# First two panels' weights in quarters ahead of their activations, and fixed orders on three engines up to the first norm's factors

## The chip, the cores and the metric

The kernel runs on one core of one Trainium2 chip. The metric is the device time of one execution in microseconds (us). The kernel before took 930.16 us (median of 3 runs, 929.11 to 930.49). TensorE is written PE below, VectorE DVE, ScalarE ACT, GpSimd POOL, and the queue that issues most transfers SP.

## The reference, cut to what matters

One layer of a hybrid decoder for 512 prompt tokens and 8 sample tokens that share the weights, all in float32. What this study touches is the first norm, the first columns of the input projection, and the rotary step on them:

```python
def rmsnorm(x, g):
    xf = x.astype(jnp.float32)
    y = xf * lax.rsqrt(jnp.mean(xf * xf, axis=-1, keepdims=True) + EPS)
    return (y * g.astype(jnp.float32)).astype(x.dtype)

def project(u, w_in, w_gk2, b_gk, pos):
    ...
    qa, ka, va, qb, kb, vb, rb, glr, ga, gb = jnp.split(u @ w_in, offs, axis=-1)
    qa = rope(qa.reshape(b, t, A_HEADS, A_HEAD_DIM), pos)
    ka = rope(ka.reshape(b, t, A_HEADS, A_HEAD_DIM), pos)
    ...
    qa, ka, va, qb, kb, vb, gk, rb, ga, gb = project(rmsnorm(xp, g_norm1[l]), w_in[l], w_gk2[l], b_gk[l], pos_p)
```

After that come windowed attention, a gated linear attention, an output projection, a second norm and a feed-forward block, none of which the change touches.

## The kernel before, in words

The 520 tokens (512 and 8) stand in columns, in two halves of 260; the 1024 features stand in 8 slices of 128 partitions, one slice being `k`. All weights are cut into panels of 128 output features; a panel is 8 tiles of 128 by 128, 512 KB, and its product is 48 matmuls: 8 slices, 2 halves, and 3 passes. The passes come from a split of every float32 operand into a high part (`whi`, `uh`) and a rest (`wlo`, `ul`): high by high, high by rest, rest by high. ACT makes the high part of a weight piece and DVE the rest (`split_piece`, L80 and L81; a piece is 4 tiles, half a panel), and the matmuls of a panel are issued by `k_tile` (L129).

The norm is not applied to the activations before the matmul. `start` multiplies the raw activations `xr` by the norm's gain only and splits them (L237 on ACT, L238 on DVE), and the matmuls of panels 0 and 1 run slice by slice as data arrive. The factor of each token, `rb`, is computed beside that in `stats`: 8 squares on ACT (L263), 7 adds on DVE (L267), a matmul with ones that sums over the partitions (L269, tile `rps`), and in `rsqrt` a logarithm and an exponential on ACT (L193, L195) with four steps of refinement on DVE (L194, L196, L197, L198). `rb` is multiplied in after the product.

Panels 0 and 1 are the two halves of the first key heads, 2 and 3 those of the first query heads, 4 and 5 the first values. `rope_pair` takes two products from PSUM: four multiplies by the cosine and sine tables (L303, L306 of the first panel, L309, L310 of the second, tile `rt`), a subtraction and an addition (L313, tile `ro`), for the keys the multiplication by `rb` (L315), and eight transfers into `KTt` or `QTt` that SP issues (L317). After the keys, `rb` is multiplied into both tables (L330), so that later pairs need no factor of their own.

Two limits of storage set the order of the work around the change. Products of panels go to the PSUM pool `pm` with two buffers (panel 2 alone has its own): panels 0, 1, 3, 4, 5 take them in turn, so panel 3 needs panel 0's product read, panel 4 panel 1's, and panel 5 that of panel 3, by its L309 and L310. Raw panels have two buffers, so the load of panel `i + 2` (L72) waits until DVE has made the last rest of panel `i`. The split weights have four buffers of half a panel, so a piece of panel `i` waits for the matmuls of panel `i - 2`.

The order of instructions on each engine is made by a scheduler that follows priorities and its own timeline. `behind` adds a constraint of order that is no wait; `after` adds a wait on a semaphore.

Of the kernel before, what the change touches and what calls it, by code (L numbers as in the profile page):

```python
# [18 lines left out]
D = 1024  # L19
# [5 lines left out]
KT = 8  # L25
# [19 lines left out]
class Build:  # L45
# [31 lines left out]
    def split_piece(self, raw, x, n, dst=None):  # L77
        nc = self.nc
        hi, lo = dst or (self.wp.tile([P, n, P], F32R, tag=t, name=t, bufs=self.wbufs) for t in ("whi", "wlo"))
        nc.scalar.activation(hi, raw[:, x:x + n], AF.Copy)  # L80
        nc.vector.tensor_tensor(lo, raw[:, x:x + n], hi.bitcast(F32), op=ALU.subtract)  # L81
        return hi, lo

    def split_panel(self, i):
# [3 lines left out]
        self.split[i] = [self.split_piece(raw, x, min(4, kt - x),  # L88
                                          i in self.wdst and [t[:, x:x + min(4, kt - x)] for t in self.wdst[i]])
                         for x in range(0, kt, 4)]  # L90
# [6 lines left out]
    def start_panels(self, panels):  # L97
        self.panels, self.raw, self.split, self.wdst, self.cur = panels, {}, {}, {}, 0
# [87 lines left out]
    def rsqrt(self, pool, out, ss, n, scale, np_=P):  # L186
# [6 lines left out]
        nc.scalar.activation(a[:np_], ss, AF.Ln, scale=scale, bias=self.eps[:np_])  # L193
        nc.vector.tensor_scalar(v[:np_], ss, scale, EPS, op0=ALU.mult, op1=ALU.add)  # L194
        nc.scalar.activation(out, a[:np_], AF.Exp, scale=-0.5)  # L195
        nc.vector.tensor_tensor(a[:np_], out, out, op=ALU.mult)  # L196
        nc.vector.scalar_tensor_tensor(a[:np_], a[:np_], -0.5, v[:np_], op0=ALU.mult, op1=ALU.mult)  # L197
        nc.vector.scalar_tensor_tensor(out, a[:np_], 1.5, out, op0=ALU.add, op1=ALU.mult)  # L198
# [7 lines left out]
    def start(self):  # L206
# [7 lines left out]
        raw = [self.raw_tile(i) for i in range(2)]  # L214

        def weights(x):
            for i in range(2):
                nc.sync.dma_start(raw[i][:, x:x + 4], self.panels[i][0][:, x:x + 4])

        nc.sync.dma_start(xr[:, 0], I["xT"][:, 0])  # L220
        weights(0)
        nc.sync.dma_start(xr[:, 1], I["xT"][:, 1])
        nc.sync.dma_start(xr[:, 2:4], I["xT"][:, 2:4])
        weights(4)
        for a in (4, 6):
            nc.sync.dma_start(xr[:, a:a + 2], I["xT"][:, a:a + 2])
# [3 lines left out]
        self.keep_warm(10)  # L230
# [5 lines left out]
        for k in range(KT):  # L236
# [977 lines left out]
```

## Time and profile before

| what | us |
|---|---|
| median of 3 runs | 930.16 |
| the profiled execution's own time | 930.86 |
| its span, first to last instruction | 929.1 |
| PE busy | 911.9 |
| DVE busy | 549.7 |
| ACT busy | 379.9 |

The span is the time between the first and the last instruction on the core in one profiled execution; the rest of its own time, 1.76 us, lies around it. Busy time of PE includes the pipelined tails of matmuls, so it is an upper account of its work. A line of the timeline stands for one instruction or for several like ones in a row: its start, the time until the last of them ends, the engine, the line of the code, what is written from what, and in brackets the idle time of the engine ahead of it and what ended that. In a row of the waits, the time is that in which the engine ahead of the arrow stood idle until the one behind it was done.

### The profile page before, as it was taken

To read this page: it belongs to the slowest core of one execution; us is meant where nothing else is said; L and a number is where in the kernel's file an instruction comes from. 1 tells how busy PE (TensorE), PEld (TensorE's weight loads), DVE (VectorE), ACT (ScalarE), POOL (GpSimd) and SP (SyncE) were. 2 spreads that over 40 slices of the span, in tenths; PEclk is the share of its full clock that TensorE was granted. 3 is DMA by queue.
4 is the path that set the end of the run, shared out by engine and by line. 5 is a ranking of instruction groups with operands and counts; after the bars stand their busy time and mean duration, and the time that the engine had idled before them with its cause. 6 is when DMAs were issued, how large, how long until landed. Compare 5 with 4: busy or idle time off the path is not lost.

```text
span 929.1 us, 19801 instructions
## 1 busy us (share of the span) xinstructions
PE 911.9 (98%) x8286; PEld 890.0 (96%) x8286; DVE 549.7 (59%) x1078; ACT 379.9 (41%) x735; POOL 66.1 (7%) x119
## 2 busy tenths in 40 slices
PE   9999999999999999999999999999999999999995
PEld 9999999999999989989999999999999999999995
DVE  6856656774966858585755555433443344555654
ACT  6234323452644445664633444322432243225432
POOL 1000000000110102010000000000000000000000
PEclk9999999999999999999999999999999999999998
DMA  7556464223544534212777767777774222223301
GB/s 250 184 180 205 128 224 174 96 75 135 205 139 141 199 104 138 74 48 98 273 272 272 272 227 273 272 272 273 272 273 159 92 91 92 91 92 114 114 32 61
DMA packets 37291, 155.27 MB, mean 167 GB/s; under 512 B 5145, under 2 KB 11553, under 8 KB 35250
## 3 DMA queue, kind: packets, MB, share of 16 engines
q1 hardware_dynamic: 32210, 95.26, 29.4%
q0 software_dynamic: 4848, 58.73, 17.8%
q8 instruction: 65, 1.06, 0.5%
q14 instruction: 24, 0.20, 0.1%
q10 hardware_dynamic: 144, 0.01, 0.0%
HBM read 140.66 MB, written 54.17 MB: 210 GB/s over the span
## 4 chain that ended last, share of the span: by engine, by line
PE 94%; DVE 2%; DMA 2%; SPq 1%; issue 0%; ACT 0%; DVEq 0%; ACTq 0%
PE mps L129 80%; PE mps L1046 5%; PE sps L384 1%; DMA QTt<-ro 1%; PE pvp L417 1%; PE lev L618 1%; PE gpo L705 1%; PE gpu L709 1%; PE ptp L401 1%; PE vps L349 1%; PE gso L772 1%; PE gpo L707 1%; DMA raw<-in_w_in 1%; SPq L317 1%; PE mps L582 0%
## 5 line engine op out<-in xcount | busy, mean ns | idle before, releaser
L80 ACT ACTIVATE whi<-raw 128x512 fp32r<-128x512 f32 x264 | 165.9, 630 | 360.8 <-PE mps L129 325.2
L81 DVE TENSOR_TENSOR wlo<-raw,whi 128x512 fp32r<-128x512 f32 x264 | 182.7, 693 | 149.4 <-ACT whi L80 145.7
L129 PE MATMUL mps<-uh,whi 128*128 128x260 f32 x928 | 193.0, 288 | 1.9 <-DVE rt L310 1.1
L129 PE MATMUL mps<-ul,whi 128*128 128x260 f32 x928 | 192.5, 286 | 0.0
L129 PE MATMUL mps<-uh,wlo 128*128 128x260 f32 x928 | 190.4, 285 | 0.0
L129 PEld LDWEIGHTS mps<-uh,whi 128*128 128x128 f32 x928 | 143.6, 189 | 4.9 <-ACT whi L80 2.4
L129 PEld LDWEIGHTS mps<-ul,whi 128*128 128x128 f32 x928 | 144.3, 189 | 2.0 <-issue 1.2
L129 PEld LDWEIGHTS mps<-uh,wlo 128*128 128x128 f32 x928 | 143.8, 188 | 1.4 <-issue 0.9
L129 PE MATMUL mps<-hh,wlo 128*128 128x260 f32 x512 | 103.2, 283 | 0.0
L129 PE MATMUL mps<-hh,whi 128*128 128x260 f32 x512 | 103.2, 283 | 0.0
L129 PE MATMUL mps<-hl,whi 128*128 128x260 f32 x512 | 103.0, 283 | 0.0
L129 PEld LDWEIGHTS mps<-hh,whi 128*128 128x128 f32 x512 | 79.0, 188 | 0.1
L129 PEld LDWEIGHTS mps<-hh,wlo 128*128 128x128 f32 x512 | 78.9, 188 | 0.0
L129 PEld LDWEIGHTS mps<-hl,whi 128*128 128x128 f32 x512 | 78.7, 188 | 0.0
L129 PE MATMUL mps<-fh,wlo 128*128 128x260 f32 x384 | 77.3, 283 | 0.0
L129 PE MATMUL mps<-fl,whi 128*128 128x260 f32 x384 | 77.2, 283 | 0.0
L129 PE MATMUL mps<-fh,whi 128*128 128x260 f32 x384 | 76.8, 282 | 0.0
L129 PEld LDWEIGHTS mps<-fh,wlo 128*128 128x128 f32 x384 | 59.2, 188 | 0.0
L129 PEld LDWEIGHTS mps<-fl,whi 128*128 128x128 f32 x384 | 59.0, 188 | 0.0
L129 PEld LDWEIGHTS mps<-fh,whi 128*128 128x128 f32 x384 | 59.0, 188 | 0.0
L1046 PE MATMUL mps<-fh,lw 128*128 128x260 f32 x256 | 46.6, 283 | 0.0
L1046 PEld LDWEIGHTS mps<-fh,lw 128*128 128x128 f32 x256 | 39.6, 188 | 0.1
(334 smaller groups left out, 1290.0 us busy)
## 6 DMA issues: line engine op xcount, KB each, us to landing
raw<-in_w_in SPq DMA_DIRECT2D x56, 512.0 KB, 3.5
raw<-in_w_up SPq DMA_DIRECT2D x32, 512.0 KB, 4.3
raw<-in_w_down SPq DMA_DIRECT2D x32, 512.0 KB, 4.7
sx<-in_state SPq DMA_DIRECT2D x8, 512.0 KB, 4.5
sx<-dV SPq DMA_DIRECT2D x8, 512.0 KB, 4.8
out_sgla<-sx POOLq DMA_DIRECT2D x8, 512.0 KB, 6.0
raw<-in_w_pb SPq DMA_DIRECT2D x8, 512.0 KB, 6.0
raw<-in_w_o SPq DMA_DIRECT2D x8, 512.0 KB, 6.0
```

Source lines behind the costliest of these rows:

```text
L80: nc.scalar.activation(hi, raw[:, x:x + n], AF.Copy)
L81: nc.vector.tensor_tensor(lo, raw[:, x:x + n], hi.bitcast(F32), op=ALU.subtract)
L129: self.last = self.nc.tensor.matmul(o[:, :HC], wt, x[:, k, j * HC:(j + 1) * HC], start=(k == 0 and n == 0), stop=(k == kt - 1 and n == 2))
L317: nc.sync.dma_start(dst[64 * (h % 2) + 32 * x:64 * (h % 2) + 32 * x + 32, gi * 2 + h // 2, :], o[32 * h:32 * h + 32, :])
L349: nc.tensor.transpose(pt[:, r * P:(r + 1) * P], vt[:, r * P:(r + 1) * P], self.c["ident"])
L384: m = nc.tensor.matmul(pss[hh][:, hp, c], Q[rows, i, b * P:(b + 1) * P], K[rows, i, ks], start=True, stop=True)
L401: nc.tensor.transpose(pt[:, hh, x], prs[hp][:, hh, x * P:(x + 1) * P], self.c["ident"])
L417: m = nc.tensor.matmul(po[64 * hh:64 * hh + 64, hp * P:(hp + 1) * P], v, pTs[hp][:, hh, x], start=(x == first), stop=(x == 1))
L618: self.nc.tensor.matmul(ps[32 * i:32 * i + 32, c], k[:, 32 * b:32 * b + 32], q[:, n * b:n * b + n], start=True, stop=True)
L705: nc.tensor.matmul(po[:, :256], ST[:, c], V[:, c], start=True, stop=(c == 0))
L707: nc.tensor.matmul(po[:, :256], qe[:, c * P:(c + 1) * P], st, start=False, stop=True)
L1046: nc.tensor.matmul(ps, w, x[:, kk, cc], start=(kk == 0 and n == 0), stop=(kk == KT - 1 and n == 2))
```

## The change

The load order on SP becomes: for each pair of slices, a quarter (2 tiles, 128 KB) of panel 0's and of panel 1's weights, then the two slices of activations one by one (the last two in one transfer). Before, halves of the panels and single or double slices alternated. ACT and DVE split the quarters as they come, so that `start` has 8 pieces of the two panels where it had 4. Eight matmuls warm PE up where ten did. In `start` the matmuls of a slice go pass by pass over both panels (high by high, rest by high, high by rest). The squares and adds move from `stats` into `start`. The helper `pin` puts every listed instruction behind the one before it on its engine, and at the end of the first `proj_qk` three written sequences carry the order on: ACT up to the first piece of panel 4, DVE through the factors' refinement, and PE, where the summing matmul stands ahead of slice 6 of panel 2 (`self.third`).

```diff
     def split_piece(self, raw, x, n, dst=None):
...
-        nc.scalar.activation(hi, raw[:, x:x + n], AF.Copy)
-        nc.vector.tensor_tensor(lo, raw[:, x:x + n], hi.bitcast(F32), op=ALU.subtract)
+        self.piece = (nc.scalar.activation(hi, raw[:, x:x + n], AF.Copy),
+                      nc.vector.tensor_tensor(lo, raw[:, x:x + n], hi.bitcast(F32), op=ALU.subtract))
...
+                if self.cur == 3 and k == 6 and n + j == 0:
+                    self.third = self.last
...
-        def weights(x):
+        last = {}
+
+        def pin(engine, m):
+
+            if engine in last:
+                self.behind(m, last[engine])
+            last[engine] = m
+
+        def load(o, i):
+            pin("SP", nc.sync.dma_start(o, i))
+
+
+        for y in range(0, KT, 2):
             for i in range(2):
-                nc.sync.dma_start(raw[i][:, x:x + 4], self.panels[i][0][:, x:x + 4])
-
-        nc.sync.dma_start(xr[:, 0], I["xT"][:, 0])
-        weights(0)
-        nc.sync.dma_start(xr[:, 1], I["xT"][:, 1])
-        nc.sync.dma_start(xr[:, 2:4], I["xT"][:, 2:4])
-        weights(4)
-        for a in (4, 6):
-            nc.sync.dma_start(xr[:, a:a + 2], I["xT"][:, a:a + 2])
+                load(raw[i][:, y:y + 2], self.panels[i][0][:, y:y + 2])
+            for k in ((y, y + 1), (y + 1, y + 2)) if y < KT - 2 else ((y, y + 2),):
+                load(xr[:, k[0]:k[1]], I["xT"][:, k[0]:k[1]])
...
-        self.keep_warm(10)
+        self.keep_warm(8)
...
+        def square():
+            k = len(sqs)
+            sqs.append(ap.tile([P, NT], F32, tag="sq", name="sq", bufs=6))
+            self.squared = nc.scalar.activation(sqs[k], xr[:, k], AF.Square)
+            pin("ACT", self.squared)
+
+        def add(k):
+            self.added = nc.vector.tensor_tensor(sqs[0], sqs[0], sqs[k], op=ALU.add)
+            pin("DVE", self.added)
+
+        for y in range(0, KT, 2):
             for i in range(2):
...
+                self.split_piece(raw[i], y, 2, [t[:, y % 4:y % 4 + 2] for t in w[i][-1]])
+                for e, m in zip(("ACT", "DVE"), self.piece):
+                    pin(e, m)
+            if y == 6:
+                square()
+                add(2)
+            for k in (y, y + 1):
+                self.split_x = nc.scalar.activation(self.uh[:, k], xr[:, k], AF.Copy, scale=self.g("n1", k))
+                pin("ACT", self.split_x)
...
+                for n in (0, 2, 1):
+                    for i in range(2):
+                        wt, x = self.passes(w[i], k, self.uh, self.ul)[n]
+                        for j in range(2):
...
+                            pin("PE", self.last)
+            if y < 6:
+                square()
+            if y == 2:
+                add(1)
+        add(3)
+        square()
+        square()
+        add(4)
...
         with self.tc.high_priority():
-            self.split_panel(2)
...
+            for x in (0, 4):
+                self.split[2].append(self.split_piece(self.raw2, x, 4))
+                for e, m in zip(("ACT", "DVE"), self.piece):
+                    pin(e, m)
+            for k in (6, 7):
+                square()
+            for k in (5, 6, 7):
+                add(k)
...
+            (a3, d3), (b3, e3) = self.pieces[3]
+            (ln, ex), m = self.rs
+
+            for seq in ([self.squared, a3, b3, ln, ex, self.pieces[4][0][0]],
+                        [self.added, *self.rt[:2], d3, m[0], e3, *m[1:], *self.rt[2:], self.pieces[4][0][1]], [self.summed, self.third]):
+                for x, y in zip(seq[1:], seq):
+                    self.behind(x, y)
```

What follows shows how the instructions stand in a row on two engines; numbers of buffers are kept where rows would read alike. On DVE, from the second multiply of the key pair's second panel to the finished factors (`rb_290`), before:

```order
L310 TENSOR_TENSOR rt_317<-mps_111,cs_242 128x520
L81 TENSOR_TENSOR wlo_411<-raw_343,whi_410 128x512
L81 TENSOR_TENSOR wlo_415<-raw_343,whi_414 128x512
L313 TENSOR_TENSOR ro_322<-rt_314,rt_316 128x512
L313 TENSOR_TENSOR ro_322<-rt_314,rt_316 128x8
L313 TENSOR_TENSOR ro_331<-rt_317,rt_315 128x512
L313 TENSOR_TENSOR ro_331<-rt_317,rt_315 128x8
L194 TENSOR_SCALAR rv_291<-rps_96 128x520
L196 TENSOR_TENSOR ra_292<-rb_290 128x520
L81 TENSOR_TENSOR wlo_490<-raw_408,whi_489 128x512
L197 SCALAR_TENSOR_TENSOR ra_292<-ra_292,rv_291 128x520
L198 SCALAR_TENSOR_TENSOR rb_290<-ra_292,rb_290 128x520
```

The same stretch of DVE now, where L345 and L348 are the four multiplies (L303, L306 of panel 0, `mps_117`, and L309, L310 of panel 1, `mps_118`, before), and L198 to L202 are the refinement:

```order
L345 TENSOR_TENSOR rt_326<-mps_117,cs_271 128x520
L345 TENSOR_TENSOR rt_327<-mps_117,sn_272 128x520
L81 TENSOR_TENSOR wlo_358<-raw_277,whi_357 128x512
L198 TENSOR_SCALAR rv_303<-rps_105 128x520
L81 TENSOR_TENSOR wlo_362<-raw_277,whi_361 128x512
L200 TENSOR_TENSOR ra_304<-rb_302 128x520
L201 SCALAR_TENSOR_TENSOR ra_304<-ra_304,rv_303 128x520
L202 SCALAR_TENSOR_TENSOR rb_302<-ra_304,rb_302 128x520
L348 TENSOR_TENSOR rt_328<-mps_118,sn_272 128x520
L348 TENSOR_TENSOR rt_329<-mps_118,cs_271 128x520
```

The refinement moved ahead of panel 1's multiplies, of the sums (L313) and of the rests of panel 4, with the two rests of panel 3 around its first step.

On DVE, the last rows up to the reading of panel 3's product (`mps_430`) now, where L353 is L313 of before, L370 is L330 and L355 is L315:

```order
L353 TENSOR_TENSOR ro_343<-rt_329,rt_327 128x8
L370 TENSOR_TENSOR cs_271<-cs_271,rb_302 128x520
L81 TENSOR_TENSOR wlo_506<-raw_420,whi_505 128x512
L355 TENSOR_TENSOR ro_334<-ro_334,rb_302 128x512
L355 TENSOR_TENSOR ro_334<-ro_334,rb_302 128x8
L355 TENSOR_TENSOR ro_343<-ro_343,rb_302 128x512
L355 TENSOR_TENSOR ro_343<-ro_343,rb_302 128x8
L345 TENSOR_TENSOR rt_414<-mps_365,cs_271 128x520
L345 TENSOR_TENSOR rt_415<-mps_365,sn_272 128x520
L81 TENSOR_TENSOR wlo_572<-raw_499,whi_571 128x512
L348 TENSOR_TENSOR rt_416<-mps_430,sn_272 128x520
L348 TENSOR_TENSOR rt_417<-mps_430,cs_271 128x520
```

Here the order is nearly as before: the tables, the multiplication by `rb` and the query pair's multiplies still follow each other, all behind the factors, with one table and two rests at other places among them.

On PE, around the matmuls that sum over the partitions, before (`mps_353` is panel 2, `mps_418` panel 3):

```order
L129 MATMUL mps_353<-uh_79,whi_252 128x260 x2
L129 MATMUL mps_353<-ul_80,whi_252 128x260 x2
L129 MATMUL mps_353<-uh_79,wlo_253 128x260 x2
L269 MATMUL rps_96<-sq_265,ones_94 128x260 x2
L129 MATMUL mps_418<-uh_79,whi_345 128x260 x2
L129 MATMUL mps_418<-ul_80,whi_345 128x260 x2
```

The same place on PE now (`mps_365` is panel 2, `mps_430` panel 3):

```order
L131 MATMUL mps_365<-uh_82,whi_283 128x260 x2
L131 MATMUL mps_365<-ul_83,whi_283 128x260 x2
L131 MATMUL mps_365<-uh_82,wlo_284 128x260 x2
L318 MATMUL rps_105<-sq_155,ones_103 128x260 x2
L131 MATMUL mps_365<-uh_82,whi_283 128x260 x2
L131 MATMUL mps_365<-ul_83,whi_283 128x260 x2
```

The sums moved from behind the last slice of panel 2 to ahead of its slice 6.

## Rows read from the trace of the kernel before

**Rows 1.** The page: span, busy times by engine, granted clock of 40 slices.
```profile
span 929.1 us, 19801 instructions
...
PE 911.9 (98%) x8286; PEld 890.0 (96%) x8286; DVE 549.7 (59%) x1078; ACT 379.9 (41%) x735; POOL 66.1 (7%) x119
...
PEclk9999999999999999999999999999999999999998
```
**Rows 2.** Waits of PE: total us, times, longest us.
```profile
PE sps L384 <- DMA QTt<-ro: 1.5, 1, 1.5
PE mps L129 <- DVE rt L310: 1.1, 1, 1.1
```
**Rows 3.** Timeline of PE: the start, panel 2's first matmuls, the sums, panel 5's first.
```profile
1.06 4.63 PE L255 MATMUL rps<-ones 128*128 128x128 f32 x20 [1.06 <-DVE eps L232]
5.34 0.78 PE L129 MATMUL mps<-uh,whi 128*128 128x260 f32 x2
...
7.35 0.50 PE L129 MATMUL mps<-uh,whi 128*128 128x260 f32 x2 [0.79 <-ACT whi L80]
7.68 0.40 PE L129 MATMUL mps<-ul,whi 128*128 128x260 f32 x2
...
18.52 0.39 PE L129 MATMUL mps<-uh,whi 128*128 128x260 f32 x2
...
24.27 1.04 PE L269 MATMUL rps<-sq,ones 128*128 128x260 f32 x4
...
37.97 0.48 PE L129 MATMUL mps<-uh,whi 128*128 128x260 f32 x2 [1.13 <-DVE rt L310]
```
**Rows 4.** Timeline of DVE, 15 to 38 us.
```profile
15.06 3.11 DVE L267 TENSOR_TENSOR sq<-sq 128x520 f32<-128x520 f32 x4 [0.30 <-ACT sq L263]
...
24.88 1.28 DVE L81 TENSOR_TENSOR wlo<-raw,whi 128x512 fp32r<-128x512 f32 x2
26.09 1.44 DVE L313 TENSOR_TENSOR ro<-rt 128x512 f32<-128x512 f32 x4
...
29.26 0.69 DVE L197 SCALAR_TENSOR_TENSOR ra<-ra,rv 128x520 f32<-128x520 f32 x1
29.99 0.70 DVE L198 SCALAR_TENSOR_TENSOR rb<-ra,rb 128x520 f32<-128x520 f32 x1
31.52 0.69 DVE L81 TENSOR_TENSOR wlo<-raw,whi 128x512 fp32r<-128x512 f32 x1 [0.84 <-ACT whi L80]
...
37.14 0.69 DVE L310 TENSOR_TENSOR rt<-mps,cs 128x520 f32<-128x520 f32 x1
```
**Rows 5.** Timeline of ACT, first 40 us.
```profile
3.80 0.73 ACT L237 ACTIVATE uh<-xr,gcols 128x520 fp32r<-128x520 f32 x1 [1.33 <-DMA gcols<-in_gcols]
4.48 0.63 ACT L80 ACTIVATE whi<-raw 128x512 fp32r<-128x512 f32 x1
6.67 0.63 ACT L80 ACTIVATE whi<-raw 128x512 fp32r<-128x512 f32 x1 [1.55 <-DMA raw<-in_w_in]
...
11.22 2.61 ACT L237 ACTIVATE uh<-xr,gcols 128x520 fp32r<-128x520 f32 x4 [0.24 <-DMA xr<-in_xT]
...
25.35 0.70 ACT L193 ACTIVATE ra<-rps,eps 128x520 f32<-128x520 f32 x1 [0.50 <-PE rps L269]
```
**Rows 6.** Transfers of the first 40 us: count, KB each, median us from issue to landing.
```profile
raw<-in_w_in SPq DMA_DIRECT2D x7, 512.0 KB, 3.3
```
**Rows 7.** Timeline of SP, first 60 us: issues of transfers.
```profile
11.41 21.16 SPq L72 DMA_DIRECT2D raw<-in_w_in  x6
32.92 5.03 SPq L317 DMA_DIRECT2D KTt<-ro  x8
...
39.80 5.95 SPq L317 DMA_DIRECT2D QTt<-ro  x8
```
**Rows 8.** Windows: stretch, length, busy PE, PEld, DVE, ACT, POOL, clock, DMA share, GB/s.
```profile
51.00:53.00 2.00, 0.50 (x5) 0.32 (x4) 0.00 (x0) 0.02 (x1) 0.00 (x0) 1.00 0.11 42
...
922.00:929.00 7.00, 0.00 (x0) 0.00 (x0) 3.10 (x6) 0.00 (x0) 0.00 (x0) 0.50 0.45 152
```

More of the change, by code (lines that the diff above doesn't have):

```diff
@@ L87, in split_panel @@
         raw = self.raw.pop(i)
-        self.split[i] = [self.split_piece(raw, x, min(4, kt - x),
-                                          i in self.wdst and [t[:, x:x + min(4, kt - x)] for t in self.wdst[i]])
-                         for x in range(0, kt, 4)]
+        self.split[i], self.pieces[i] = [], []
+        for x in range(0, kt, 4):
+            self.split[i].append(self.split_piece(raw, x, min(4, kt - x),
+                                                  i in self.wdst and [t[:, x:x + min(4, kt - x)] for t in self.wdst[i]]))
+            self.pieces[i].append(self.piece)
     def passes(self, w, k, xh, xl):
@@ L97, in start_panels @@
     def start_panels(self, panels):
-        self.panels, self.raw, self.split, self.wdst, self.cur = panels, {}, {}, {}, 0
+        self.panels, self.raw, self.split, self.wdst, self.cur, self.pieces = panels, {}, {}, {}, 0, {}
     def panel_mm(self, xh, xl, pool=None):
@@ L204, in g, with start @@
         return self.c["gcols"][:, o:o + 1]
-    def start(self):
+    def start(self, ap):
         nc, I = self.nc, self.I
@@ L250, in start @@
+        self.sum = sqs[0]
         return xr, [p[:, :, :HC] for p in ps]
@@ L255, in keep_warm, with stats @@
             self.nc.tensor.matmul(self.warm[:, 0, :P], self.ones, self.ones, start=True, stop=True)
-    def stats(self, ap, xr):
-        nc = self.nc
-        pr = self.warm
-        acc = None
-        for k in range(KT):
-            a = ap.tile([P, NT], F32, tag="sq", name="sq", bufs=6)
-            self.after(nc.scalar.activation(a, xr[:, k], AF.Square), self.split_x)
-            if acc is None:
-                acc = a
-            else:
-                self.added = nc.vector.tensor_tensor(acc, acc, a, op=ALU.add)
+    def stats(self, ap):
+        nc, pr, acc = self.nc, self.warm, self.sum
         for j in range(2):
-            nc.tensor.matmul(pr[:, j, :HC], self.ones, acc[:, j * HC:(j + 1) * HC], start=True, stop=True)
+            self.summed = nc.tensor.matmul(pr[:, j, :HC], self.ones, acc[:, j * HC:(j + 1) * HC], start=True, stop=True)
         self.rb = self.t("rb", bufs=1)
-        self.rsqrt(ap, halves(self.rb), pr[:, :, :HC], NT, 1 / D)
+        self.rs = self.rsqrt(ap, halves(self.rb), pr[:, :, :HC], NT, 1 / D)
     def late_consts(self):
@@ L865, in run @@
         self.rp = rp.enter_context(tc.tile_pool(name="rp", **right))
-        xr, first = self.start()
+        stp = ExitStack()
+        p = stp.enter_context(tc.tile_pool(name="stp", **right))
+        xr, first = self.start(p)
         self.oa = self.cp.tile([P, 2, NT], F32, tag="oa", name="oa")
```

54 lines of the change are left out of this document (26 added, 28 removed).

## The prediction

> **What bounds the kernel now.** Read the page first: PE is busy 911.9 of 929.1 us [rows 1], so the end can only move by what PE idles or runs slowly, and the waits of PE say where. Within the first 60 us there are two large ones: 1.5 us for the query transfers (`QTt`) and 1.1 us for a multiply of the query pair (L310) [rows 2]. A third lies at the start: the first real matmul starts at 5.34, and a pause of 0.79 us ends at 7.35 with the split of panel 1's weights [rows 3]. Then read PE's timeline for three marks: panel 2 starts at 18.52, the summing matmuls at 24.27, and panel 5 at 37.97 behind its wait for L310 [rows 3]. So panel 2's 48 matmuls take 24.27 - 18.52 = 5.75 us, 0.12 each, and panels 2 to 4 with the sums are worked through at 37.97 - 1.13 = 36.84, after 18.3 us. Last, read DVE, for which PE waits there: it works through from 31.52 to the end of L310 at 37.14 + 0.69 = 37.83 [rows 4]. PE got to panel 5 at 36.84 and stood until 37.97. **The start is bounded by loads and splits, but its end is handed over by DVE.** That is the point on which the change must be judged: how early panel 2 starts counts for nothing if DVE reads panel 3's product no sooner.
>
> **The start, until panel 2.** The first matmul needs ACT's high parts of both quarters and of slice 0. The gain columns land at 3.80, when ACT's wait for them ends [rows 5], and that transfer is not changed. Slice 0 now lies behind two quarters: the first 516 KB instead of the first 260. Before, the second transfer, which ends with the same 516 KB, was split from 4.48 on without a wait [rows 5]. So slice 0 is split between 3.80 and 4.5, 0.73 each, and the first matmul starts between 4.6 and 5.3; I take 5.1, since eight warm-up matmuls end 4.63 x 8/10 = 3.7 us after 1.06, at 4.8, and are no bar. At the start PE runs at the lower of its two levels, 1.2 GHz: twenty passes of 128 columns take 4.63 us there, 0.22 each, as long as passes of 260 columns at 24.27 (1.04 for four that overlap) [rows 3], though the row of granted clock shows nothing of it [rows 1]. By 7.68 two matmuls show 0.40, the figure of full speed. So the 12 matmuls of slice 0, at twice 0.12 until about 7.0, end near 7.5. Slice 1 is then due, with 776 KB loaded; before, the transfer that ended with 772 KB landed at 6.67 [rows 5], so slice 1 is split at 6.7 to 7.4: just in time. The other seven slices take 7 x 12 x 0.12 = 10.1 us: **panel 2 could start at 17.6 instead of 18.52**.
>
> What must hide: the last slices, due at 7.5 + 5 x 1.44 = 14.7. Before, ACT split slices 4 to 7 from 11.22 to 13.83 [rows 5], the last two from about 12.5. The same bytes come in more, smaller pieces; the cover is 14.7 - 12.5 - 0.7 for the split, 1.5 us. ACT's own work for a pair of slices is two quarters (half of 0.63 each), two slices of 0.63 (2.61 for four) and a square, no longer than a slice: some 2.5 us, against 2.9 us of PE: hidden. The split in quarters costs DVE some 0.1 us for each of four more instructions, in a stretch where it waits for data: nothing.
>
> Panel 2's load waits for DVE's last rest of panel 0, and that now comes with slices 6 and 7: at about 13.2 instead of 11.4 [rows 7]. A 512 KB load lands 3.3 us after its issue [rows 6]: 16.5, then 0.63 of ACT: 17.2, ahead of 17.6 by 0.4 us. If it is later than that, panel 2 slips one for one.
>
> **The sums and factors.** The summing matmuls start after 36 of panel 2's matmuls: 17.6 + 4.3 = 21.9. The adds are ready: dependent ones take 0.8 us each (3.11 for four) [rows 4], five of them remain after the last slice's rest (15.5), with two rests of panel 2 between: 15.5 + 5 x 0.8 + 1.2 = 20.7. The logarithm starts 25.35 - 24.27 = 1.08 us after the sums [rows 3, 5], so at 23.0, and ends at 23.7. Until then DVE stands idle for about 1.2 us, because its fixed order puts the first refinement step next and this follows the logarithm. Before, DVE had work there.
>
> **DVE from 23.7 to panel 3's product.** Now count rows of the order: an independent instruction of 512 or 520 columns takes 0.61 from start to start (1.28 for two), a dependent one 0.73 (29.26 to 29.99) [rows 4]. First step, rest, square: 1.8. Two dependent steps: 1.5. Panel 1's multiplies: 1.2. Two rests: 1.2. Two sums, two tables, two rests: 1.4 + 1.2 + 1.2. The keys times the factors: 1.4. Query multiplies with one rest between, the last counted to its end: 1.2 + 0.6 + 0.6 + 0.7. Sum 14.0, so DVE has read panel 3's product at **37.7**, and panel 5 starts 0.14 later as before, at 37.85 against 37.97. PE has done panel 4 at 17.6 + 18.3 = 35.9 and waits 2 us instead of 1.13. The 0.9 us won at the front goes into that wait: factors come some 3.7 us earlier (27.0 against 30.69), but they were not what DVE lacked; its work behind them is the same, and an idle 1.2 us took the place of one of 0.84 (at 31.52). Gain: **0.1 us**. A place later, `QTt`'s transfers are issued from 39.80 on behind DVE's query sums and the eight transfers of `KTt`, which take SP 5.03 us from 32.92 [rows 7]. The keys are now ready 1.0 us later, at about 33.9, so SP is through at 39.0 and with panel loads at 39.4, 0.4 us ahead of need. The wait of 1.5 us thus keeps its length; its bounds are 0, if the queries meet less traffic, and 2.0 if SP is late by 0.5. Behind it both orders are the same.
>
> **The rivals.** (a) **The front's gain reaches the end**, which needs DVE to be through by 36.9 or earlier and `QTt` to land without a wait. The first matmul cannot start before 3.80 + 0.73, so panel 2 not before 17.1 and panel 5 not before 37.3: 0.65 us, plus the whole 1.5 us: 2.15 us, 928.0. For it: transfers of keys move away from those of queries. Against it: the 14.0 us are counted in instructions.
> (b) **PE's clock falls in the longer wait**, on the other side. The clock stayed full in every slice but the last [rows 1], also where PE was busy only 0.50 of 2 us [rows 8]; after PE's last work it was at 0.50, the level of 1.2 GHz [rows 8]. The new pause of 2 us is longer than any that the trace shows survived. A fall costs half of the time for which it lasts; at the start the lower level lasted from 1.06 to about 7, so 3.0 us at most and 1.5 for half of that: 931.6 to 933.1. It decides from a pause beyond 1.5 us. The Trainium skill ("TensorE: Matmul & The Clock Gate", section "HAM oscillation — how this bites in real kernels") warns of just this, that waits for data between bursts of matmuls bring the clock down again and the next burst starts slow. By that rule the sum would be that of this rival; the pauses of 1.13 and 1.5 us in the trace do not show it.
> (c) **Data come late in quarters.** A weight's run within a partition falls from 2 KB to 1 KB. No row shows the price. The 1 MB of the two panels is a third of the 3.1 MB that were in by about 12.5 us, so it took at most 4.2; between no loss and half as much again lie 0 and 2.1 us, of which 1.5 are covered. The slow landing at 6.67, though, has no cover: slice 1 and panel 2's load (cover 0.4) pass each us on. I take 0, and 1.5 us as the far end: 931.6, with a late `QTt` 932.1. The Trainium skill ("Perfetto Trace Analysis", section "DMA Optimizations") says that transfers under 2 KB carry a notable overhead, and beside it that smaller pieces may let work start sooner. By the first, this rival would hold; no row here shows it either way.
> (d) **The front does not move**, since loads set the pace as before: panel 2 at 18.5, panel 5 at 38.8: 0.8 us slower, still no change that can be told.
>
> **How the numbers follow.** The profiled execution took 930.86 us, 0.70 above the median of 930.16. Its own sum is 930.86 - 0.1 = 930.75, and on the median's scale 930.05: I say 930.1. A measurement of this kernel can tell 0.2%, 1.9 us, from no change: below 928.3 or above 932.0. The forecast and (d) hold 0.69 between them, (a) 0.16, (b) 0.08 and (c) 0.07. Of (a) I put 0.12 below 928.3, since it needs nearly all of its 2.15 us, though runs of one kernel scatter by 1.4 us; of (b) and (c), 0.11 above 932.0. So faster 0.12, slower 0.11, same 0.77. The range reaches from near (a)'s bound into (b)'s span and to (c)'s far end: 928.2 to 932.2.
>
> **What would show it.** In the profile after: the first real matmul near 5.1, panel 2 near 17.6, sums near 21.9, DVE idle about 1.2 us ahead of the first refinement step, the factors done near 27.0, the last query multiply ending near 37.7, panel 5 near 37.9 with PE's largest wait there some 2 us. Wrong would be: panel 5 before 37.0, or a granted clock of 0.5 in a slice near 38 us, or an end that moves while panel 5 does not.

## The result, and the profile after

The changed kernel took 932.47 us (median of 22 executions, 931.11 to 936.04) where the kernel before took 930.48 beside it: a ratio of 1.0022, with a 95% interval of 1.0012 to 1.0032. It is slower, by 0.2%, and the time lies 0.27 us outside the predicted range. (The ratios compare undisturbed executions that ran beside each other and are not quotients of the medians; the two can differ by some 0.8 us.)

The page of after, first lines and the granted clock, beside [rows 1]:

```profile
span 932.9 us, 19812 instructions
...
PE 912.8 (98%) x8282; PEld 890.4 (95%) x8282; DVE 550.1 (59%) x1082; ACT 379.8 (41%) x739; POOL 65.9 (7%) x119
...
PEclk9999999999999999999999999999999999999998
```

The waits of PE in its first 62 us (total, times, longest):

```profile
PE sps L424 <- DMA QTt<-ro: 2.2, 2, 1.8
PE mps L131 <- DVE rt L348: 1.9, 1, 1.9
PE mps L277 <- ACT uh L269: 1.6, 1, 1.6
```

Its timeline of PE, beside [rows 3]: the first real matmul, panel 2, the sums, panel 5, the scores (`sps`) that need the query transfers.

```profile
6.36 0.75 PE L277 MATMUL mps<-uh,whi 128*128 128x260 f32 x4 [1.63 <-ACT uh L269]
6.95 0.65 PE L277 MATMUL mps<-uh,wlo 128*128 128x260 f32 x4
...
18.27 0.51 PE L131 MATMUL mps<-uh,whi 128*128 128x260 f32 x2
...
22.94 1.04 PE L318 MATMUL rps<-sq,ones 128*128 128x260 f32 x4
...
38.86 0.48 PE L131 MATMUL mps<-uh,whi 128*128 128x260 f32 x2 [1.93 <-DVE rt L348]
...
51.89 0.69 PE L424 MATMUL sps<-KTt,QTt 64*128 64x128 f32 x4 [0.37 <-DMA QTt<-ro]
54.42 0.56 PE L424 MATMUL sps<-KTt,QTt 64*128 64x128 f32 x4 [1.85 <-DMA QTt<-ro]
```

The timeline of DVE around the idle stretch and at the end of its count, beside [rows 4]:

```profile
18.25 1.29 DVE L81 TENSOR_TENSOR wlo<-raw,whi 128x512 fp32r<-128x512 f32 x2 [1.10 <-ACT whi L80]
...
24.75 0.70 DVE L198 TENSOR_SCALAR rv<-rps 128x520 f32<-128x520 f32 x1 [1.17 <-ACT ra L197]
...
38.03 0.69 DVE L348 TENSOR_TENSOR rt<-mps,cs 128x520 f32<-128x520 f32 x1
```

Stretches of the same execution (length; busy time of PE, PEld, DVE, ACT, POOL; granted clock; DMA share; GB/s):

```profile
39.40:42.80 3.40, 3.40 (x31) 3.40 (x30) 2.19 (x7) 0.82 (x2) 0.55 (x1) 1.00 0.71 183
...
55.70:59.10 3.40, 3.40 (x18) 3.40 (x17) 2.57 (x12) 1.65 (x8) 0.00 (x0) 0.50 0.29 90
59.10:62.00 2.90, 2.90 (x26) 2.90 (x26) 0.69 (x1) 0.63 (x1) 0.00 (x0) 1.00 0.41 123
```

From 55.70 to 59.10 PE does 18 matmuls, where the stretch of the same length from 39.40 holds 31. Behind the wait for `QTt` the clock fell to 0.50, the level of 1.2 GHz, and that cost 1.6 us. The 40 slices of the page are too wide to show it.

The profiled execution of before took 930.86, above its median, and that of after 934.64, far above its own. So more profiled executions of both stand beside them here. Marks on PE, in us:

| | before | before again | after | after again | after, third |
|---|---|---|---|---|---|
| panel 2 starts | 18.52 | 18.10 | 18.27 | 18.70 | 18.29 |
| panel 5 starts | 37.97 | 37.90 | 38.86 | 39.29 | 38.88 |
| last wait for QTt | 1.5 | none | 1.85 | none | 1.68 |
| scores start behind it | 52.69 | 51.07 | 54.42 | 53.40 | 53.21 |
| clock at 0.50 ahead of 62 us | no | no | 55.7 to 59.1 | 39.4 to 42.8 | no |
| last matmul starts | 919.86 | 918.20 | 923.52 | 921.34 | 921.47 |
| its own time | 930.86 | 929.22 | 934.64 | 932.45 | 932.62 |

The second of before took 1.3 us less than the median of 930.48, but only 0.3 less than the 929.54 of the executions beside it; the last two of after are near its median.

Which of these is the common case can be read from the mean granted clock, which is on record for all executions of after and of the runs below, not only for the profiled ones. In the eighteen profiles of this study the mean is 0.996 or 0.997 where the clock never falls to 0.50 ahead of the last matmuls, 0.994 or 0.995 where it falls once, and 0.992 or 0.993 where it falls twice. By this reading the clock fell in 27 of the 35 executions of after, and in 15 of the 120 of before. In before a fall shows in the time: a median of 932.35 with one, 929.66 without. In after it does not: 932.5 with one and 932.5 in the eight without. Where in an execution the fall lies, the mean does not tell.

### The profile page after: what moved, and what is told of

Its sections match the earlier page's. It is cut to its first block, busy times and chain, and to the rows that moved or that the text cites. A ratio compares the mean times of both kernels' runs of the same rounds, so it can differ in the third digit from the quotient of the medians.

```text
span 932.9 us, 19812 instructions
## 1 busy us (share of the span) xinstructions
PE 912.8 (98%) x8282; PEld 890.4 (95%) x8282; DVE 550.1 (59%) x1082; ACT 379.8 (41%) x739; POOL 65.9 (7%) x119
## 4 chain that ended last, share of the span: by engine, by line
PE 93%; DVE 3%; DMA 2%; issue 1%; ACT 0%; SPq 0%; DVEq 0%; ACTq 0%
PE mps L131 78%; PE mps L1096 5%; DMA raw<-in_w_in 1%; PE sps L424 1%; DMA QTt<-ro 1%; PE pvp L457 1%; PE lev L658 1%; PE gpo L745 1%; PE gpu L749 1%; PE ptp L441 1%; PE vps L389 1%; PE gso L812 1%; PE gpo L747 1%; DVE wlo L81 1%; DMA xr<-in_xT 1%
## 5 line engine op out<-in xcount | busy, mean ns | idle before, releaser
L80 ACT ACTIVATE whi<-raw 128x512 fp32r<-128x512 f32 (+1 forms) x268 | 166.3, 623 | 356.9 <-PE mps L131 323.2
L81 DVE TENSOR_TENSOR wlo<-raw,whi 128x512 fp32r<-128x512 f32 (+1 forms) x268 | 183.0, 685 | 148.3 <-ACT whi L80 145.6
L131 PE MATMUL mps<-uh,whi 128*128 128x260 f32 x896 | 187.9, 289 | 2.1 <-DVE rt L348 1.9
L131 PE MATMUL mps<-ul,whi 128*128 128x260 f32 x896 | 186.4, 287 | 0.0
L131 PE MATMUL mps<-uh,wlo 128*128 128x260 f32 x896 | 184.2, 286 | 0.0
L131 PEld LDWEIGHTS mps<-uh,whi 128*128 128x128 f32 x896 | 139.6, 189 | 5.0 <-issue 3.9
L131 PEld LDWEIGHTS mps<-ul,whi 128*128 128x128 f32 x896 | 139.8, 189 | 2.0 <-issue 1.2
L131 PEld LDWEIGHTS mps<-uh,wlo 128*128 128x128 f32 x896 | 139.3, 189 | 1.6 <-issue 0.9
```

The costliest lines, as they stand in the source:

```text
L80: self.piece = (nc.scalar.activation(hi, raw[:, x:x + n], AF.Copy), nc.vector.tensor_tensor(lo, raw[:, x:x + n], hi.bitcast(F32), op=ALU.s ...
```

## The experiments

The theory at the outset (F) was the prediction's own chain, a front that is later than summed and handed over by DVE. Its rivals were the written orders (O), the quarters (Q), the clock behind longer waits (C) and the tail, that is the transfers of `QTt` (T, later K).

**What in the change does it.** The written sequences left out:

```diff
-            for seq in ([self.squared, a3, b3, ln, ex, self.pieces[4][0][0]],
...
-                for x, y in zip(seq[1:], seq):
-                    self.behind(x, y)
```


> Theory F (front): the kernel after lost 0.9 us at panel 5 because the load of panel 2 landed late (17.48, panel 2 at 18.27 where 17.6 was forecast) and DVE's count of 14.0 us from the logarithm on handed that over; a later wait for QTt added 0.8. This run keeps the load order and the orders pinned in the start, and leaves out the three written sequences at the end of the first key pair. F expects panel 2 still near 18.3 and panel 5 between 38.3 and 38.9, so no more than 0.6 us of the 2.0 us back: ratio to the kernel before 1.0015 to 1.0025. Theory O (orders): the written sequences are to blame, since they leave DVE idle for 1.17 us ahead of the first refinement step where the scheduler had found work; then panel 5 starts near 37.7 (38.86 - 1.17) and the ratio is 1.000 to 1.001.

Measured: 935.43 us, 1.0067 (1.0055 to 1.0079). Both theories missed it: panel 5 at 38.87 as theory F had it, but for another reason (it waited for `vt`, not for the query multiplies, which ended only at 41.75), since the scheduler now put the sums behind panel 3 (30.11) and the query multiplies behind the keys. So PE waited 3.26 us for `QTt`, and the clock fell behind that. The written sequences are not the loss; without them the kernel is some 3 to 4 us worse.

The quarters alone, in the kernel before:

```diff
-        weights(0)
...
+        for y in range(0, KT, 2):
+            for i in range(2):
+                nc.sync.dma_start(raw[i][:, y:y + 2], self.panels[i][0][:, y:y + 2])
```


> The kernel before, with the load order of after (quarters of the two panels ahead of the slices), the split in quarters and eight warm-up matmuls, and nothing else. Theory Q (quarters): loads in quarters are to blame, by late slices or by the later load of panel 2; then panel 2 starts at 18.5 or later, panel 5 at 38.5 or later (0.5 us or more behind 37.97), and the ratio is 1.001 to 1.003, all of the loss that shows ahead of 40 us. Theory O (the pinned and written orders are to blame): panel 5 within 0.2 us of 37.97, ratio 0.9995 to 1.0005.

Measured: 931.08 us, 1.0013 (1.0004 to 1.0022), panel 5 at 38.35, between the two theories. PE waits twice for splits of panel 2 (0.38 each, at 18.14 and 19.26). With the earlier load order come the splits in quarters and two warm-up matmuls fewer; together they cost some 0.4 us at panel 5. Of the 1.2 us in the ratio (0.4 to 2.0) another 0.3 is a wait for `QTt`. The profiled execution, the longest of the eleven, adds a long multiply on POOL (last section).

Panel 2's load freed, in the kernel after:

```diff
-        self.load_panel(2)
+        self.raw[2] = self.big("raw2")[:, :, :P]
+        self.nc.sync.dma_start(self.raw[2], self.panels[2][0])
```


> The kernel after, but panel 2's raw weights get a place of their own, so that their load no longer waits for DVE's last rest of panel 0. Theory F expects the steps as forecast for the change: panel 2 at 17.5 to 17.7 (18.27 in after), the summing matmuls at 21.8 to 22.1, the last query multiply ending 37.6 to 38.0 (38.72), panel 5 at 37.8 to 38.1 (38.86), and with it 0.8 to 1.0 us of the 2.0 back at least: ratio 1.000 to 1.0012. Rival S: the splits of the last slices or the adds, not the load, held panel 2 and the sums; then panel 2 stays at 18.2 to 18.3, panel 5 at 38.7 to 38.9, ratio 1.0022.

Measured: panel 2 at 17.70, sums at 21.99, the last query multiply done at 37.77, panel 5 at 37.91: each mark of theory F, and of the forecast for the change itself. And yet 932.13 us, 1.0027 (1.0017 to 1.0037). The front's lateness was taken away and the time stayed. Panel 2 in its timeline, then its windows, which say why (the wait at panel 5 was 1.94 us; columns as above):

```profile
17.70 0.40 PE L131 MATMUL mps<-uh,whi 128*128 128x260 f32 x2
...
36.00:39.20 3.20, 1.29 (x11) 1.32 (x12) 3.20 (x7) 0.40 (x1) 0.46 (x1) 1.00 0.51 138
39.20:42.60 3.40, 3.40 (x18) 3.40 (x17) 1.45 (x6) 0.18 (x1) 1.17 (x3) 0.50 0.88 249
42.70:46.00 3.30, 3.30 (x30) 3.30 (x30) 0.75 (x2) 1.08 (x3) 0.00 (x0) 1.00 1.02 347
```

The clock fell behind the wait at panel 5: panel 5 took 7.84 us to panel 6 and not 6.3. This is rival (b), place and price. By the mean clock all eight executions had a fall.

DVE's idle stretch filled:

```diff
-                        [self.added, *self.rt[:2], d3, m[0], e3, *m[1:], *self.rt[2:], self.pieces[4][0][1]], ...
+                        [self.added, *self.rt, d3, m[0], e3, *m[1:], self.pieces[4][0][1]], ...
```


> The kernel after, with one change of the written order of DVE: panel 1's two multiplies come ahead of the first refinement step, where DVE stood idle for 1.17 us, and not behind the last. Theory F (what DVE does behind the logarithm, in instructions, sets panel 5): the last query multiply ends 1.2 us earlier at 37.5, panel 5 at 37.65, and the transfers of the keys are issued some 1.2 us earlier too; time 1.2 us less than after if the query transfers follow, ratio 1.0005 to 1.0015. Rival T (tail): the query transfers land at 54.4 whatever the front does, because they are limited by traffic; then the wait for QTt grows by what panel 5 gains, and the ratio stays 1.002.

Measured: 930.00 us, 1.0011 (0.9998 to 1.0023). Panel 5 at 36.91, 1.95 us earlier than in after and without a wait, since the scheduler moved the key sums into the idle stretch too; the wait for `QTt` was 1.89 us, with a fall of the clock behind it (52.73 to 56.14). So in this execution part of the gain went to the tail, as rival T said. But it is the longest of the twelve (935.35), with a second fall at 414.54. Eight of the twelve had no fall by the mean clock, and their median is 929.52; how long they waited for `QTt` is not on record.

**Is it the clock?** Filling the idle time of PE keeps the clock up without making anything earlier.

```diff
+            for _ in range(7 if i == 4 else 0):
+                self.last = self.behind(nc.tensor.matmul(ps[:, 0, 384:512], self.ones, self.ones, start=True, stop=True),
+                                        self.last)
```


> The kernel with a place of its own for panel 2's weights (profiled at 931.74, with panel 5 at 37.91 as forecast, and the clock at 0.5 from 39.21 to 42.63), plus seven matmuls of ones by ones on PE between panels 4 and 5, about 1.5 us of work in the wait of 1.94 us; their result is not used. Theory C: no fall near 39 us, panel 6 begins 6.2 to 6.3 us after panel 5 and not 7.8, and the time is 1.0 to 1.6 us below that kernel's 932.13: 930.5 to 931.1, ratio 1.001 to 1.0017. Rival N: the fall has another cause than the idle wait; then it stays, and the ratio stays 1.0027.

Measured: 931.60 us, 1.0015 (1.0005 to 1.0025). On the clock theory C held: no fall in the profile, and by the mean clock a fall in one execution of eleven, against eight of eight without the busy matmuls. On the time it fits (that kernel had 1.0027), but the two intervals overlap. In the profiled execution PE was late to full speed at the start (last section).

> The kernel after, unchanged, for a second profile of it beside the kernels of this call. Theory C (clock): each wait of about 2 us of PE that the new order makes (1.93 us at panel 5, 1.85 us for QTt) may bring the granted clock to 0.5 for a stretch that costs 1.6 us, and the first profile shows only one of the ways this goes; C expects a fall to 0.5 again within a few us of one of the two waits, though not necessarily the same one, and a ratio of 1.002. Theory F (front) holds without any fall: panel 5 at 38.7 to 38.9 and QTt 0.8 us later than in the kernel before, 1.0018 with no fall in the first 60 us.

Measured: 932.52 us, 1.0029 (1.0018 to 1.0039). The fall is at the other wait this time, in the timeline of PE and in the windows:

```profile
39.29 0.65 PE L131 MATMUL mps<-uh,whi 128*128 128x260 f32 x2 [1.93 <-DVE rt L348]
```

```profile
39.40:42.80 3.40, 3.40 (x17) 3.40 (x18) 2.62 (x9) 0.00 (x0) 0.74 (x2) 0.50 0.70 169
42.80:46.20 3.40, 3.40 (x30) 3.40 (x30) 0.69 (x1) 1.12 (x2) 0.88 (x2) 1.00 1.04 353
```

PE then came to the scores at 53.40 and found `QTt` landed: the slow stretch had used up that wait.

```diff
+                if first:
+                    for _ in range(6):
+                        m = nc.tensor.matmul(pss[1][:, 0, :P], self.ones, self.ones, start=True, stop=True)
+                        prev = self.behind(m, prev or self.last)
```


> The kernel after with seven such matmuls between panels 4 and 5 and six ahead of the first score matmuls, in its two waits; their results are not used. Theory C: no fall in the first 60 us, the wait for QTt still ends near 54.4, and the time is below that of the kernel after in the same call by the share of its executions that fall times 1.6 us: 0.5 to 1.6 us, ratio 1.0005 to 1.0015. Theory F: falls are rare in the kernel after, so the time stays within 0.4 us of it, ratio 1.002.

Measured: 932.81 us, 1.0021 (1.0008 to 1.0033). Theory C's half on the clock held (no fall up to the end), its half on the time did not: the scores still started at 53.19 to 54.03. By the mean clock none of the twelve executions fell, and they are no faster. Without the fall PE simply waits for `QTt`.

The scores behind one more panel, in the kernel with the multiplies first:

```diff
-        self.fill(self.rate)
+        self.fill(self.rate if self.cur > 7 else 0)
```


> The kernel with panel 1's multiplies ahead of the refinement (930.0), plus the first matmuls of the scores moved behind one more panel, so that QTt has landed when PE needs it. Its profile had panel 5 at 36.91, a wait of 1.89 us for QTt and a fall of the clock behind it. Theory F and C: no wait for QTt, no fall there, PE 1.9 to 3.5 us earlier from panel 8 on: 926.5 to 928.1, ratio 0.997 to 0.9985. Rival T: the wait only moves to the next thing that PE needs from a transfer or from ACT (the scores' exponentials, ptp, stand one panel later too); then the time stays at 930, ratio 1.000 to 1.001.

Measured: 930.60 us, 1.0003 (0.9991 to 1.0015). No wait for `QTt`, but 1.79 us for the values' transposes at 83.86 and a fall behind it: rival T. This too is an execution far above the median (933.15); eight of eleven had no fall by the mean clock, with a median of 929.87.

Both kernels unchanged:

> The kernel before, unchanged, one more look: its profiled execution of 930.86 lay above its median. Theory C2 (the clock in both kernels): the kernel before has no fall to 0.5 in its first 60 us (waits of 1.1 to 1.5 us only), the clock rises near 7 us, panel 2 starts at 18.4 to 18.6 and panel 5 at 37.9 to 38.1, in this execution too; what varies is the wait for QTt, between 0.3 and 1.5 us. Rival: it falls at the QTt wait or rises late too; then falls are no difference between the two kernels.

> The kernel after, unchanged, a third profile. Theory C2: a fall to 0.5 in the first 60 us again, at panel 5 or behind the wait for QTt, and panel 5 at 38.7 to 39.4; if the clock rises late at the start (near 10 us, as two profiles of edited kernels showed it), panel 2 starts at 19.5 to 19.7. Rival: no fall and panel 5 at 38.8; then the two falls that the profiles showed are not typical.

Measured: 929.22 and 932.62 us, both without a fall. PE's waits in the first 62 us of before again, and then the timeline of PE at the scores in after's third execution:

```profile
PE mps L129 <- DVE rt L310: 1.1, 1, 1.1
PE rps L255 <- DVE eps L232: 1.1, 1, 1.1
PE mps L129 <- ACT whi L80: 0.8, 1, 0.8
```

```profile
53.21 1.17 PE L424 MATMUL sps<-KTt,QTt 64*128 64x128 f32 x8 [1.68 <-DMA raw<-in_w_in]
```

The kernel before does not wait for `QTt` in this execution, and 105 of its 120 have no fall. (The row of after names a panel load; what the scores read is `KTt` and `QTt`, and the sixth transfer of `QTt`, which the first scores need, lands at 53.08 by the transfers' records.) So C2 is right for before. For after this profile is as its rival had it, but it is one of the eight in 35: most executions do fall, as C2 said. The fall alone still does not make the difference, since the eight take as long.

```diff
-        self.keep_warm(8)
+        self.keep_warm(11)
```


> The kernel after with eleven warm-up matmuls in place of eight, so that PE is not idle between 4.9 and the first real matmul at 5.9 to 6.4. Theory W (start): part of the executions of the kernel after find the clock still at the lower level until about 10 us, since PE stands idle for 1.1 to 1.6 us ahead of slice 0, and lose 1.3 us at panel 2; then this kernel is 0.3 to 0.8 us faster than after, with the clock up before 6.5 us: ratio 1.0012 to 1.002. Rival: the start does not matter, because panel 2's load (landing at 17.5) and the wait at panel 5 take any gain: ratio 1.0022 to 1.0029 as after.

Measured: 932.67 us, 1.0038 (1.0022 to 1.0053). Theory W falls: the clock was up at 6.9, yet panel 2 came at 18.25 and panel 5 at 38.83, as in after.

**Why QTt comes late.** Timelines of SP and of POOL in before again:

```profile
32.85 5.02 SPq L317 DMA_DIRECT2D KTt<-ro  x8
...
39.73 6.08 SPq L317 DMA_DIRECT2D QTt<-ro  x8
```

```profile
40.44 0.54 POOL L480 DMA_DIRECT2D kcb<-in_kc  x1
```

The same in after's third execution:

```profile
35.06 5.03 SPq L357 DMA_DIRECT2D KTt<-ro  x8
...
40.81 5.84 SPq L357 DMA_DIRECT2D QTt<-ro  x8
```

```profile
42.20 0.54 POOL L375 DMA_DIRECT2D out_kT<-KTt  x1 [1.94 <-DMA KTt<-ro]
42.73 0.54 POOL L520 DMA_DIRECT2D kcb<-in_kc  x1
```

The keys are 2.2 us later, `QTt` is issued 1.1 later, and the 1 MB load of `kcb`, which stands on POOL behind the keys' output, 2.3 later. The last `QTt` lands at 53.8, not 51.4. In the kernel before, the load held back:

```diff
-            nc.gpsimd.dma_start(kc, I["kc"][:, gi])
+            m = nc.gpsimd.dma_start(kc, I["kc"][:, gi])
+            if gi == 0:
+                self.after(m, self.hold)
```


> The kernel before, with one edit: the 1 MB load of kcb waits for panel 5's last matmul (44.1) and so starts some 3.7 us later than 40.4, in the midst of QTt's transfers; the scheduler then sets the first score matmuls 4 matmuls (0.5 us) earlier, as the kernel after has them. Theory K (collision): QTt lands at 52.8 to 54, 1.5 to 2.5 us later than 51.4, PE waits 1.5 us or more for it, panel 5 stays at 37.9, and the time rises by 1.5 to 2.8 us: ratio 1.0015 to 1.003. Rival P (panel 5): what the kernel after lost, it lost through panel 5 and the clock; then kcb's place does not matter, ratio 0.9995 to 1.0005.

Measured: 929.70 us, 1.0001 (0.9992 to 1.0011). The held-back load came behind the transfers, not among them: seven of the eight had landed by 46.9, where 50.6 stood in before again. So the collision is there in before too (3.7 us), but costs nothing, since PE does not need `QTt` sooner. The run does not decide between K and P.

In the kernel after, the load held back further:

```diff
+            if gi == 0:
+                self.after(m, self.last)
```


> The kernel after, with the 1 MB load of kcb held back until panel 6's last matmul (about 51), behind QTt. Theory K: QTt lands at 50.5 to 51.7 and not at 53.4 to 54.4, the wait of 1.7 to 1.9 us goes down to 0.3 or less, panel 5 stays at 38.8; time 1.4 to 1.9 us below the kernel after: ratio 1.0005 to 1.0012, the rest being panel 5. Rival P: the time stays at 1.0022 to 1.0029.

Measured: 932.71 us, 1.0034 (1.0022 to 1.0046). `QTt` had landed by 49.5 and PE did not wait for it; theory K's time failed all the same. The transfers from 38 to 52 us (KB each, median us from issue to landing), after's third execution and then this one:

```profile
QTt<-ro SPq DMA_DIRECT2D x8, 65.0 KB, 8.3
```

```profile
QTt<-ro SPq DMA_DIRECT2D x8, 65.0 KB, 5.0
```

Its waits and windows show what took the place (four of the five executions fell by the mean clock; the profiled one, the longest, fell again at 133.3):

```profile
PE mps L131 <- DVE rt L348: 1.9, 1, 1.9
```

```profile
41.20:44.50 3.30, 3.30 (x17) 3.30 (x16) 1.25 (x6) 0.38 (x1) 0.54 (x1) 0.50 0.83 254
```

That edit together with the seven busy matmuls between panels 4 and 5:

> The kernel after with kcb's load held back behind panel 6 (so that QTt lands near 49.5) and the seven matmuls of ones by ones between panels 4 and 5 (so that PE is not idle there; their result is not used). Theory E (either one costs): no fall, no wait for QTt, and 1.4 to 1.9 us less than after's 932.5: what is left to the kernel before is panel 5, 0.9 to 1.3 us later: ratio 1.001 to 1.0015. Rival: taking both away gives nothing either, ratio 1.002 to 1.003; then the loss lies behind 60 us.

Measured: 0.9999 (0.9988 to 1.0011), medians 930.48 and 929.83. PE's only wait between 8 and 62 us, and two stretches behind it:

```profile
PE mps L135 <- DVE rt L354: 0.4, 1, 0.4
```

```profile
41.20:44.50 3.30, 3.30 (x30) 3.30 (x30) 2.08 (x7) 1.21 (x2) 1.10 (x2) 1.00 0.79 174
44.60:48.00 3.40, 3.40 (x31) 3.40 (x30) 1.45 (x4) 0.63 (x1) 0.54 (x1) 1.00 0.97 374
```

Theory E held, and more than it said: with both away the time is that of before within its interval, which leaves room for 1 us either way. The four kernels side by side, each with its ratio to before and the executions that fell by the mean clock (the kernel at the lower left has busy matmuls ahead of the scores too):

| | QTt late | QTt landed early |
|---|---|---|
| PE idle ahead of panel 5 | 1.0022 and 1.0029; 27 of 35 | 1.0034; 4 of 5 |
| PE kept busy there | 1.0021; 0 of 12 | 0.9999; 1 of 12 |

**A faster kernel.** Where DVE's idle stretch is filled, panel 5 does not wait, and with `QTt` out of the load's way there is no wait left for the clock to fall in. The edits are those shown above, three together and then two.

> Three edits of the kernel after together: panel 2's weights in a place of their own, panel 1's multiplies ahead of the refinement, kcb's load behind panel 6. Theory K with F: panel 2 at 17.7, panel 5 at 36.0 without a wait, QTt landed by 49.5, no wait of PE over 0.5 us between 8 and 60 us, and PE 1.9 to 2.2 us ahead of the kernel before from panel 6 on: ratio 0.9975 to 0.9985. Rival: another wait behind 60 us takes the gain (the values' transposes at 131, the key load for the samples): ratio 0.9995 to 1.000.

Measured: 928.27 us, 0.9988 (0.9979 to 0.9998). Panel 5 at 36.39, `QTt` landed by 48.3, no wait of PE over 0.35 us between 8 and 60; the gain is 1.3 us, not the 1.9 to 2.2 expected.

> The kernel of the three edits without the first: panel 2's weights share the two places again, so that panel 2 starts at 18.2 or later and the sums near 22.9. Theory F (DVE hands its lateness over): the factors and with them panel 5 come 0.5 to 0.9 us later than in the kernel of three edits (36.9 where that had 36.4 with a start 0.6 us late), and the time is 0.4 to 0.9 us above its 928.27: ratio 0.9992 to 0.9998. Rival: the load of panel 2 is hidden once panel 5 does not wait; then the ratio is 0.9985 to 0.999.

Measured: 928.29 us, 0.9980 (0.9971 to 0.9988), faster than both kernels; none of its twelve executions fell. Its rival was right: once panel 5 does not wait, panel 2's load no longer counts. PE's only wait between 8 and 62 us:

```profile
PE mps L131 <- ACT whi L80: 0.2, 1, 0.2
```

## Why the prediction was wrong

**The first matmul (5.1; came at 5.8 to 6.4).** The sum let slice 0 be in by 3.80, because the second transfer of before, ending at the same 516 KB, had been split without a wait [rows 5]. Slice 0 is now the third transfer, and ACT waited for it until 5.58. Part of that came back: the clock was up by then, so the 12 matmuls of slice 0 took 1.5 us, not 2.4.

**Panel 2 (17.6; came at 18.3).** The term that was mis-sized is the landing of its load: 3.3 us, the median of seven [rows 6], for a transfer that took 4.2 (issued 13.37, ACT began at 17.58). The cover of 0.4 us was gone, and as the prediction said, panel 2 then slipped: 0.7 us at its start, and 1.0 at the sums (22.94 for 21.9), since its first pairs of matmuls followed each other at 0.34 to 0.38 and not at 0.24. With the load freed, panel 2 started at 17.70.

**DVE's count (14.0 us; right).** From 24.75 to 38.03 + 0.69 are 13.97 us; the idle stretch ahead of it was 1.17 for 1.2, the wait at panel 5 1.93 for 2. So panel 5 came at 38.86 for 37.85, with all of the lateness of panel 2's load; with that load freed it came at 37.91. This part of the prediction was right by its mechanism.

**The wait for QTt (said to keep its 1.5 us; the step that failed, together with the weight of rival (b)).** The 1.5 us [rows 2] belonged to one execution, 0.70 above the median; before again has none. Taken as part of the kernel, it made the base too slow there, and hid what the change adds. Three things add: the keys, put 1.0 us later in the sum, were 2.2 later, of which 1.0 is panel 2's load handed on (with it freed they are issued at 34.09, for 33.9 in the sum, and `QTt` at 39.83 as in before); `kcb`'s load moved with them into the queries' transfers, which the prediction did not follow though it stands on POOL behind the keys' output; and "behind it both orders are the same" was not so: the scores stand behind 21 matmuls after the values' transposes where 26 stood before, so PE needs `QTt` 0.6 us sooner. The last two hold without panel 2's lateness: with its load freed the sixth transfer landed at 51.75, and PE, which came at 52.03 only because of its fall, would have come some 1.5 us sooner and waited 1.2 (an estimate from these marks).

Between two executions without a fall, before again and after's third, the last matmul moved by 921.47 - 918.20 = 3.27 us: 0.98 at panel 5, 1.68 for `QTt`, 0.37 in a wait at L812 (0.70 where 0.33 was), and 0.24 not assigned. What moved L812 was not tried. In the commoner case, after again with a fall at panel 5, it moved by 3.14 us: 1.39 at panel 5 and 1.54 in the slow stretch to panel 6 make 2.93 of them, and the wait for `QTt` is gone. These are differences of single executions; between the medians lie 2.0 to 2.5 us.

**Rival (b), given 0.08.** The time came out in its span (931.6 to 933.1), and most executions of after had a fall. The mechanism was real: a wait of 1.93 us at panel 5 and a clock of 0.50 behind it, 1.5 us lost, the lower end of its price. The place was right in after again and with panel 2's load freed; in the first profile of after the fall came one wait later. The Trainium skill ("TensorE: Matmul & The Clock Gate", section "HAM oscillation — how this bites in real kernels") warns that waits for data between bursts make the next one start slow; the traces agree, with waits of 1.79 to 1.94 us ahead of a fall in five kernels, and the prediction weighed it too low because only survived waits of 1.13 and 1.5 stood in its rows. But the price does not add to that of `QTt`: a fall at panel 5 uses up the later wait, and without the fall the wait is there. That is why each repair of after alone gave nothing and both together gave the loss back, as far as the interval tells. What the 0.65 us between the medians of the last is made of, panel 5 or chance, stays open.

**Rival (c)** was right in kind: the quarters alone cost 0.4 us at panel 5 and 1.2 in the time (0.4 to 2.0), so its far end of 1.5 is not excluded. They are no fixed price, for the two fastest kernels have them too. The Trainium skill ("Perfetto Trace Analysis", section "DMA Optimizations") has transfers under 2 KB carry a notable overhead; the run with the quarters alone agrees in sign, and does not tell overhead from the changed order of landing.

## What to carry to other kernels

A wait read from one profiled execution may belong to that execution: where its time lies above the median, look again before a sum is built on it. When two waits follow each other on one engine, a delay at the first fills the second, so an experiment that takes one away proves nothing until both are gone. And a wait that grows beyond what the trace has shown survived is priced with the clock behind it, even where the instruction count says the front gains; the better edit gives the idle engine work, as the reordered multiplies did.

## What the runs showed of the hardware that was not expected

The same wait of 1.93 us at panel 5 brought the clock down in one profiled execution of after and not in two others, and a wait of 2.9 us (below) did so in two kernels and not in a third, so its length alone does not decide. The stretches at 0.50 ahead of the last matmuls are each 3.4 us long in the profiles.

PE comes up to full speed at the start at different moments though the program is the same up to there (the row of granted clock does not show this, the matmuls' own times do). In the kernel with both waits away slice 0 ran at half rate (1.07 us for four matmuls, against 0.65 in after at 6.95), which put panel 2 at 19.63:

```profile
5.89 1.23 PE L283 MATMUL mps<-uh,whi 128*128 128x260 f32 x4 [1.05 <-ACT uh L275]
6.92 1.07 PE L283 MATMUL mps<-uh,wlo 128*128 128x260 f32 x4
...
10.38 0.77 PE L283 MATMUL mps<-ul,whi 128*128 128x260 f32 x4
```

Four of the edited kernels showed this, up to about 10 us; no execution of before or after in the table had it past about 7.

One multiply on POOL took 3.88 us in three profiles (the quarters alone here) where it takes 1.6 in the others (before again here), and PE waited 2.9 us for it and not 0.6 and 0.8; nothing in the edits touches it. That is 1.5 us in such an execution, and in two of the three the clock fell behind it. What goes with it shows on DVE: where POOL took 3.88, DVE's multiplies of 256 columns beside it all took 0.42; in the fifteen other profiles two of these took 1.5. So the two engines hold each other up there, and one or the other loses; what decides which stays open.

```profile
406.82 3.88 POOL L641 TENSOR_TENSOR kl<-kl,QKb 128x512 f32<-128x512 f32 x1 [16.95 <-ACT kl L640]
...
407.21 0.42 DVE L659 TENSOR_TENSOR D<-D,QKb 128x256 f32<-128x256 f32 x1
```

```profile
406.05 1.62 POOL L645 TENSOR_TENSOR kl<-kl,QKb 128x512 f32<-128x512 f32 x1 [16.95 <-ACT kl L644]
...
406.45 1.51 DVE L663 TENSOR_TENSOR D<-D,QKb 128x256 f32<-128x256 f32 x1
```
